# A hybrid decoder layer on one core: 1/rms in the projection's input, evictions on ScalarE, tail copies on GpSimd, log1p as a product of quadratics

## Chip, cores, metric

One Trainium2 chip, one core. The metric is the device time of one execution in microseconds; the time before is 2660.73 us, the median of three runs (2657.97 to 2662.61). The profile is of one execution. Engines: PE is TensorE (PEld its weight loads), DVE is VectorE, ACT is ScalarE, POOL is GpSimd, SP issues the DMAs.

## What is computed

One decoder layer over 16 meta tokens and 2048 real tokens of width 1024, in float32, batch 1:

```
h    = rmsnorm(x, norm1_g);  proj = h @ w_in            # one projection, 3608 columns
qkv  = silu(causal_conv(proj[q, k, v], conv_w))         # 4 taps, 1536 channels
gated delta rule, 4 heads of 128 (chunked)              # log decay: -exp(a_log) * softplus(...)
g    = log_sigmoid(glr @ gla_w2 + gla_b) / 16           # glr: 16 columns of proj; g: 256 channels
gated linear attention, 4 heads (chunked, cumsum of g)
x    = x + concat(rmsnorm(o) * silu(gate)) @ w_out
x    = x + square(relu(rmsnorm(x) @ w_up)) @ w_down     # 4096 wide
out  = rmsnorm(x, final_norm_g)
```

The log of a sigmoid is computed as min(x, 0) - log1p(e) with e = exp(-|x|), and log1p on [0, 1] as e times a polynomial of degree 9.

## The kernel before

Matmuls keep float32 accuracy by splitting each operand into a high and a low part: `mm3` (lines 117 to 119) issues three matmuls, high times high, high times low and low times high. `wchunk` (L95) loads 256 rows of weights, ScalarE casts the high part `whi` (L101), and VectorE, or GpSimd for two chunks of four in the projection, subtracts it for the low part `wlo` (L102). `split` (L107) does the same for activations (`hh` and `hl`, lines 112 and 113).

The program runs in this order: projection of token blocks 0 and 1 (`phase_a`, blocks of 512 tokens), the scans over pairs of chunks of 128 tokens woven with blocks 2 and 3, and then the output projection and the MLP (`phase_c`) of blocks 0, 1 and last 2 and 3 together. The blocks are numbered 0 to 3, as in the code. A scheduler sets each engine's order from the dependences, priorities and its own estimates of durations, so that work of the scans stands between the matmuls of the projection. Every engine works its own queue in order.

`phase_a` has eight groups per block (`group`, L232). A group takes four PSUM banks `pa`, four chunks of weights (kk) and 24 matmuls of each chunk (four banks, two rows of 128 weights, three parts): 96 matmuls. First one token group, then three convolution groups (`conv_group`, q, k and v channels on the partitions), one group for q and k of the gated linear attention, and three token groups. At a group's end each bank is evicted: token groups by ScalarE with 1/rms as a scale on the partition (`evac_tok`, L336), channel groups by VectorE with 1/rms along the free dimension, `rb` (`evac_c`, L409, tile `craw`; `evac_g`, L375, tile `gqk`). 1/rms comes from `stats` (L191), in the same block's first group, since the input itself is only multiplied by the gain (`normless`, L168). After a convolution group, for each bank, VectorE copies three columns in front of the new block from `tails` and three of its end into `tails` (lines 416 and 417), ScalarE does the first tap (L419, tile `cy`) and VectorE the other three (L421), then a silu.

The pool of banks has four buffers. The jobs of `decays` (L352) run in small parts between the groups and take a bank each: `pglr`, `pgc`, `pgr`, `pgla`. So at a group's end TensorE goes on only when banks have been evicted, and the buffers go round. `gla_decay` (L310) evaluates log1p (L157) by Horner's rule on VectorE: one product and nine steps of 512 columns.

The scan's inverse of 32 x 32 blocks is a chain of some 60 VectorE instructions per pair of chunks (`inv_t`, `inv_v`, lines 564 and 570), followed by two levels of small matmuls with copies between them (`wt`, lines 586 and 606).

## Time and profile before

| | |
|---|---|
| median of three runs | 2660.73 us |
| span of the profiled execution | 2658.3 us |
| TensorE busy | 2569.2 us (97%) |
| VectorE busy | 1625.0 us (61%) |
| ScalarE busy | 905.4 us (34%) |
| GpSimd busy | 475.8 us (18%) |
| mean granted TensorE clock | 0.986 |

The profiled execution's own time is its span and the little that lies around it; the page gives only the span, and the median of the runs stands 2.4 us above it. The share of busy time is an average over stages. Rows name a line of the kernel, the engine, the operation and the tiles (out<-in, buffer numbers left out). A wait names the instruction that ended last.

### The profile page before, as it was taken

How to read it: one execution, taken by the hardware profiler on the slowest of the kernel's cores; microseconds unless marked ns; L12 is line 12 of the kernel's file. 1: busy time of each engine (PE TensorE's matmuls, PEld its weight loads, DVE VectorE, ACT ScalarE, POOL GpSimd, SP SyncE). 2: the span in 40 equal slices, each digit the busy share in tenths (PEclk: the TensorE clock that was granted, in tenths of full speed). 3: DMA queues.
4: the chain of work that ended last, by engine and by line, in shares of the span. 5: the costliest groups of instructions: out<-in, count | busy, mean ns of one | idle time of the engine just before them, and what ended most of it. 6: DMA issues, size and time to landing. Idle time of an engine off the chain costs nothing.

```text
span 2658.3 us, 35430 instructions
## 1 busy us (share of the span) xinstructions
PE 2569.2 (97%) x13426; PEld 2127.1 (80%) x13426; DVE 1625.0 (61%) x3122; ACT 905.4 (34%) x1850; POOL 475.8 (18%) x385
## 2 busy tenths in 40 slices
PE   8999999999899999999998999999999999999998
PEld 6788688789678778888786888888888888888887
DVE  4777866985984875857679567555453343233335
ACT  4344345345334433334353243333321122112212
POOL 2123123223222321102044020101230000000003
PEclk9999999999999999999999999999999999999999
DMA  5264455355346323334363343253211111111111
GB/s 180 102 214 146 139 152 182 111 187 174 126 154 201 103 89 124 104 106 127 115 208 94 100 121 105 86 175 108 98 48 48 48 48 48 48 48 48 48 48 64
DMA packets 187122, 297.30 MB, mean 112 GB/s; under 512 B 33584, under 2 KB 116104, under 8 KB 186952
## 3 DMA queue, kind: packets, MB, share of 16 engines
q1 hardware_dynamic: 186952, 295.05, 35.5%
q8 instruction: 105, 1.72, 0.3%
q14 instruction: 65, 0.53, 0.1%
HBM read 244.62 MB, written 50.37 MB: 111 GB/s over the span
## 4 chain that ended last, share of the span: by engine, by line
PE 63%; DVE 9%; issue 2%; DMA 2%; POOL 1%; ACT 0%; SPq 0%; POOLq 0%; DVEq 0%; ACTq 0%
PE pc L119 18%; PE pc L118 18%; PE pc L117 18%; PE pa L117 2%; PE pa L118 2%; PE pa L119 2%; DVE wlo L102 1%; DVE inv_t L564 1%; DVE inv_v L570 1%; PE pks L650 1%; DVE l1p L163 0%; PE po L661 0%; PE pu L664 0%; PE po L660 0%; PE py L654 0%
## 5 line engine op out<-in xcount | busy, mean ns | idle before, releaser
L101 ACT CAST whi<-wraw 128x1024 fp32r<-128x1024 f32 (+1 forms) x344 | 346.9, 1009 | 1067.8 <-PE pc L118 813.0
L102 DVE TENSOR_TENSOR wlo<-wraw,whi 128x1024 fp32r<-128x1024 f32 (+1 forms) x280 | 344.8, 1232 | 576.3 <-ACT whi L101 575.2
L118 PE MATMUL pc<-avl,whi 128*128 128x512 f32 (+1 forms) x1056 | 413.1, 391 | 2.5 <-DVE avl L110 2.4
L117 PE MATMUL pc<-avh,whi 128*128 128x512 f32 (+1 forms) x1056 | 397.4, 392 | 12.2 <-DVE acc L974 12.0
L119 PE MATMUL pc<-avh,wlo 128*128 128x512 f32 (+1 forms) x1056 | 406.7, 389 | 0.0
L117 PE MATMUL pc<-h2h,whi 128*128 128x512 f32 x1024 | 402.0, 393 | 2.8 <-DVE acc L896 2.8
L118 PE MATMUL pc<-h2l,whi 128*128 128x512 f32 x1024 | 402.7, 393 | 0.0
L119 PE MATMUL pc<-h2h,wlo 128*128 128x512 f32 x1024 | 399.1, 396 | 1.1 <-DVE wlo L102 1.1
L117 PEld LDWEIGHTS pc<-avh,whi 128*128 128x128 f32 x1056 | 199.6, 189 | 57.3 <-issue 13.3
L118 PEld LDWEIGHTS pc<-avl,whi 128*128 128x128 f32 x1056 | 199.4, 189 | 47.1 <-DVE avl L110 4.8
L119 PEld LDWEIGHTS pc<-avh,wlo 128*128 128x128 f32 x1056 | 199.4, 189 | 42.8
L883 POOL TENSOR_TENSOR tot<-tot,sqk 128x512 f32<-128x512 f32 (+1 forms) x63 | 84.5, 1347 | 824.3 <-ACT sqk L882 822.5
L117 PEld LDWEIGHTS pc<-h2h,whi 128*128 128x128 f32 x1024 | 192.5, 188 | 46.1 <-DVE acc L896 4.1
L119 PEld LDWEIGHTS pc<-h2h,wlo 128*128 128x128 f32 x1024 | 192.3, 188 | 44.4 <-DVE wlo L102 1.9
L118 PEld LDWEIGHTS pc<-h2l,whi 128*128 128x128 f32 x1024 | 192.4, 188 | 42.6
L974 DVE TENSOR_TENSOR acc<-acc,pc 128x512 f32<-128x512 f32 x240 | 162.2, 685 | 104.3 <-PE pc L119 101.9
L102 POOL TENSOR_TENSOR wlo<-wraw,whi 128x780 fp32r<-128x780 f32 (+1 forms) x64 | 142.9, 2233 | 433.2 <-ACT whi L101 345.0
L117 PE MATMUL pa<-hh,whi 128*128 128x512 f32 x512 | 206.6, 405 | 4.2 <-ACT whi L101 2.3
L118 PE MATMUL pa<-hl,whi 128*128 128x512 f32 x512 | 202.7, 396 | 0.0
L119 PE MATMUL pa<-hh,wlo 128*128 128x512 f32 x512 | 188.8, 400 | 2.0 <-DVE wlo L102 1.2
L117 PE MATMUL pa<-whi,hh 128*128 128x390 f32 x512 | 167.8, 357 | 13.8 <-ACT hh L112 11.2
L118 PE MATMUL pa<-wlo,hh 128*128 128x390 f32 x512 | 180.4, 354 | 0.1
(274 smaller groups left out, 4079.7 us busy)
## 6 DMA issues: line engine op xcount, KB each, us to landing
wraw<-in_wup_dram SPq DMA_DIRECT2D x96, 512.0 KB, 3.6
wraw<-in_wdn_dram SPq DMA_DIRECT2D x96, 512.0 KB, 3.6
wraw<-in_wch_dram SPq DMA_DIRECT2D x64, 512.0 KB, 3.7
wraw<-in_wtk_dram SPq DMA_DIRECT2D x64, 390.0 KB, 3.9
qkv_d<-cy SPq DMA_DIRECT2D x48, 256.0 KB, 2.3
kqv<-qkv_d SPq DMA_DIRECT2D x16, 768.0 KB, 5.3
wraw<-in_wo_dram SPq DMA_DIRECT2D x24, 512.0 KB, 3.6
xk<-in_xT_dram SPq DMA_DIRECT2D x32, 256.0 KB, 4.2
```

What stands on the lines that cost most here:

```text
L101: A.copy(out=hi[:, :, 0:n], in_=raw[:, :, 0:n])
L102: eng.tensor_tensor(out=lo[:, :, 0:n], in0=raw[:, :, 0:n], in1=hi[:, :, 0:n].bitcast(F32), op=ALU.subtract)
L117: T.matmul(o, lhsT=ah, rhs=bh, start=first, stop=False)
L118: T.matmul(o, lhsT=ah, rhs=bl, start=False, stop=False)
L119: T.matmul(o, lhsT=al, rhs=bh, start=False, stop=last)
L564: V.tensor_tensor(out=t, in0=vv[:, 0:c, c : c + 1].broadcast_to([L, c, n]), in1=vv[:, c : c + 1, c + 1 : w].broadcast_to([L, c, n]), op=AL ...
L570: V.tensor_tensor(out=vv[:, 0:c, c + 1 : w], in0=vv[:, 0:c, c + 1 : w], in1=t, op=ALU.add)
L650: T.matmul(h4(pk)[:, h, :], lhsT=kg[:, h, :], rhs=S[:, h, :], start=True, stop=True)
L883: eng.tensor_tensor(out=tot, in0=tot, in1=sq, op=ALU.add)
L974: V.tensor_tensor(out=x, in0=x, in1=banks[j][i], op=ALU.add)
```

## The change

In blocks 1 to 3 the input is multiplied by gain and 1/rms on VectorE before it is split, so that evictions need no factor; ScalarE evicts channel banks there. The row sums of the next block are taken after the fourth group of the block before. GpSimd copies the convolution's tails, with two buffers of tails. log1p of the linear attention's gates becomes a product of one linear and four quadratic factors: ScalarE squares, VectorE multiplies. Block 0 keeps its evictions.

```diff
+_roots = np.roots(LOG1P[::-1])
+LR = float(_roots[np.abs(_roots.imag) < 1e-9].real[0])
+LA = [float(-z.real) for z in _roots if z.imag > 1e-9]
+LB = [float(z.imag**2) for z in _roots if z.imag > 1e-9]
+LC = LOG1P[-1]
...
+    lsc = [(-LC) ** 0.5, 1.0, 1.0, 1.0]
+    lbias = const("lbias", [128, 4])
+    for i in range(4):
+        G.memset(lbias[:, i : i + 1], lsc[i] * LA[i])
...
+    norms = {}
+    def stats(b):
+        rt = wk.tile([128, 4], F32, name="rt", tag="rt")
+        rb = wk.tile([128, 512], F32, name="rb", tag="rb")
...
+        A.copy(out=rb, in_=pb)
+        norms[b] = rt, rb
...
+        told, tnew = tails[b % 2], tails[(b + 1) % 2]
...
-        def normless(k):
+        def moving(k):
             if k not in hT:
                 xk = t512("xk")
                 nc.sync.dma_start(out=xk, in_=I["xT"][b, k])
                 hT[k] = act("h")
-                split(xk, *hT[k], g1[:, k : k + 1])
+                if meta:
+                    split(xk, *hT[k], g1[:, k : k + 1])
+                else:
+                    V.scalar_tensor_tensor(out=xk, in0=xk, scalar=g1[:, k : k + 1], in1=norms[b][1], op0=ALU.mult, op1=ALU.mult)
+                    split(xk, *hT[k])
             return hT[k]
...
-                x = t512("glx")
-                V.tensor_scalar(out=x[:, 0:n], in0=px[:, 0:n], scalar1=gb[:, j : j + 1], scalar2=None, op0=ALU.add)
-                e = t512("gle")
...
-                l = yield from log1p(e[:, 0:n], 128, [512] if n == 512 else [n], f"l1p_{n}")
-                V.scalar_tensor_tensor(out=x[:, 0:n], in0=x[:, 0:n], scalar=0.0, in1=l[:, 0:n], op0=ALU.min, op1=ALU.subtract)
-                V.tensor_tensor_scan(out=dst[j], data0=rmask[:, 0:n], data1=x[:, 0:n], initial=0.0, op0=ALU.mult, op1=ALU.add)
+                x = dst[j]
+                V.tensor_scalar(out=x, in0=px[:, 0:n], scalar1=gb[:, j : j + 1], scalar2=None, op0=ALU.add)
+                e, y = tl("gle"), tl("gly")
+                A.activation(out=e, in_=x, func=AF.Abs)
+                A.activation(out=e, in_=e, func=AF.Exp, scale=-1.0)
+                V.scalar_tensor_tensor(out=y, in0=e, scalar=-LR, in1=e, op0=ALU.add, op1=ALU.mult)
+                for i in range(4):
+                    yield False
+                    sq = tl("gls")
+                    A.activation(out=sq, in_=e, func=AF.Square, scale=lsc[i], bias=lbias[:, i : i + 1])
+                    V.scalar_tensor_tensor(out=y, in0=sq, scalar=lsc[i] ** 2 * LB[i], in1=y, op0=ALU.add, op1=ALU.mult)
+                V.scalar_tensor_tensor(out=y, in0=x, scalar=0.0, in1=y, op0=ALU.min, op1=ALU.add)
+                V.tensor_tensor_scan(out=x, data0=rmask[:, 0:n], data1=y, initial=0.0, op0=ALU.mult, op1=ALU.add)
...
         def evac_tok(t, pt):
             st = av("tok")
-            A.activation(out=st[:, 0:NTOK], in_=pt[:, 0:NTOK], func=AF.Copy, scale=rt[:, t : t + 1])
+            if meta:
+                A.activation(out=st[:, 0:NTOK], in_=pt[:, 0:NTOK], func=AF.Copy, scale=norms[0][0][:, t : t + 1])
+            else:
+                A.copy(out=st[:, 0:NTOK], in_=pt[:, 0:NTOK])
...
         def evac_g(j, pt):
...
+                A.activation(out=st[:, 0:TB], in_=pt, func=AF.Copy, scale=scale)
...
             def evac_c(j, pt):
                 raw = av("craw")
-                V.tensor_tensor(out=raw[:, 3 : TB + 3], in0=pt, in1=rb, op=ALU.mult)
+                if meta:
+                    V.tensor_tensor(out=raw[:, 3 : TB + 3], in0=pt, in1=norms[0][1], op=ALU.mult)
+                else:
+                    A.copy(out=raw[:, 3 : TB + 3], in_=pt)
...
-                V.tensor_copy(out=raw[:, 0:3], in_=tails[:, m, :])
-                V.tensor_copy(out=tails[:, m, :], in_=raw[:, TB : TB + 3])
+                G.tensor_copy(out=raw[:, 0:3], in_=told[:, m, :])
+                if b + 1 < NB:
+                    G.tensor_copy(out=tnew[:, m, :], in_=raw[:, TB : TB + 3])
...
         group(I["wch"][3], 512, True, evac_g, done_g, 512 if meta else 0, meta_g)
+        if b + 1 < NB:
+            stats(b + 1)
...
-                m = tail.tile([128, 512], F32, name="mixk", tag="mixk", bufs=4) if tail else t512("mixk")
+                m = tail.tile([128, 512], F32, name="mixk", tag="mixk", bufs=3) if tail else t512("mixk")
```

The scheduler orders the whole program anew. Three places show what moved.

VectorE, end of the second convolution group of block 2, before (`pa` are the group's banks, `cy` the taps of the group before, `inv` the inverse of the chunk pair):

```order
L102 TENSOR_TENSOR wlo_5290<-wraw_5287,whi_5289 128x1024
L564 TENSOR_TENSOR inv_t_4196<-inv_v_4195 32x220
L426 SCALAR_TENSOR_TENSOR cy_5079<-cth_5084,cy_5079 128x512
L411 TENSOR_TENSOR craw_5219<-pa_5088,rb_4667 128x512
L416 COPY craw_5221<-tails_137 128x3
L570 TENSOR_TENSOR inv_v_4195<-inv_v_4195,inv_t_4196 32x11x20
L411 TENSOR_TENSOR craw_5221<-pa_5089,rb_4667 128x512
L416 COPY craw_5223<-tails_137 128x3
L417 COPY tails_137<-craw_5219 128x3
L411 TENSOR_TENSOR craw_5223<-pa_5090,rb_4667 128x512
```

The same group's end in the change, on ScalarE:

```order
L112 CAST whi_5221<-wraw_5219 128x1024
L467 ACTIVATE cth_5118<-cy_5113 128x512
L112 CAST whi_5322<-wraw_5320 128x1024
L452 COPY craw_5253<-pa_5122 128x512
L452 COPY craw_5255<-pa_5123 128x512
L452 COPY craw_5257<-pa_5124 128x512
L112 CAST whi_5355<-wraw_5353 128x1024
L452 COPY craw_5259<-pa_5125 128x512
L351 ACTIVATE gle_5267<-bb_4921 128x512
```

The evictions of this group went from VectorE's queue, between taps and inverse, to ScalarE's, three of them ahead of the cast of the next group's second chunk (`whi_5355`).

GpSimd in the change, between the weights of this group and those of the next (`wlo_5356` is the low part of that second chunk; before, the rows `wlo` of the two groups followed each other there):

```order
L113 TENSOR_TENSOR wlo_5191<-wraw_5188,whi_5190 128x1024
L457 COPY craw_5255<-tails0_142 128x3
L459 COPY tails1_143<-craw_5253 128x3
L457 COPY craw_5257<-tails0_142 128x3
L459 COPY tails1_143<-craw_5255 128x3
L457 COPY craw_5259<-tails0_142 128x3
L459 COPY tails1_143<-craw_5257 128x3
L457 COPY craw_5454<-tails0_142 128x3
L113 TENSOR_TENSOR wlo_5356<-wraw_5353,whi_5355 128x1024
```

Seven tail copies came in between two weight subtractions.

VectorE at the start of block 2 in the change (`xk` is the input, `rb` 1/rms, `Sg`, `gqg` and `f_u` belong to the scan; before, the two `hl` followed on their casts without a product ahead):

```order
L211 SCALAR_TENSOR_TENSOR xk_4735<-xk_4735,g1_135,rb_2846 128x512
L211 SCALAR_TENSOR_TENSOR xk_4745<-xk_4745,g1_135,rb_2846 128x512
L827 SCALAR_TENSOR_TENSOR Sg_124<-Sg_124,gall_3949,pgu_3987 64x128 x4
L783 TENSOR_SCALAR gqg_4346<-gqg_4346,eb_4341 128x64 x2
L93 TENSOR_SCALAR f_u_4002<-ms_3997 128x4
L211 SCALAR_TENSOR_TENSOR xk_4779<-xk_4779,g1_135,rb_2846 128x512
L121 TENSOR_TENSOR hl_4738<-xk_4735,hh_4737 128x512
L121 TENSOR_TENSOR hl_4748<-xk_4745,hh_4747 128x512
```

Each `xk` is now multiplied first, then cast by ScalarE, then subtracted.

## Rows read from the trace of the kernel before

**Rows 1.** The page's busy table: busy us, share of the span, instructions.
```profile
PE 2569.2 (97%) x13426; PEld 2127.1 (80%) x13426; DVE 1625.0 (61%) x3122; ACT 905.4 (34%) x1850; POOL 475.8 (18%) x385
```
**Rows 2.** Busy time of each engine by stretch: the four blocks of the projection, and the time from the output projection on. Columns: stretch in us, its length, busy us of each engine with its instructions, mean granted TensorE clock, DMA share, GB/s.
```profile
0.00:240.00 240.00, 223.53 (x1236) 187.71 (x1237) 161.76 (x379) 104.03 (x212) 61.85 (x52) 0.97 0.52 166
240.00:430.00 190.00, 176.76 (x969) 148.56 (x969) 143.95 (x289) 73.01 (x140) 51.85 (x38) 0.96 0.48 149
430.00:640.00 210.00, 200.55 (x1195) 174.83 (x1195) 170.09 (x363) 95.00 (x233) 64.80 (x47) 0.98 0.51 158
640.00:850.00 210.00, 194.30 (x1079) 164.71 (x1079) 159.10 (x321) 81.22 (x165) 50.22 (x35) 0.97 0.48 150
850.00:2600.00 1750.00, 1727.90 (x8644) 1409.38 (x8644) 962.60 (x1715) 538.63 (x1074) 226.23 (x193) 1.00 0.30 92
```
**Rows 3.** What TensorE waited for, 0 to 850 us: us in total, times, longest.
```profile
PE pa L117 <- ACT hh L112: 11.2, 6, 6.2
PE pr L614 <- DVE wt L606: 5.7, 2, 3.0
PE pgc L301 <- DVE craw L411: 5.4, 3, 2.5
PE pgla L322 <- DVE craw L411: 4.3, 2, 2.2
...
PE pa L117 <- DVE tails L417: 1.9, 4, 0.7
```
**Rows 4.** VectorE in order of time at the end of the second convolution group of block 2: start us, us, instruction, and the idle time before it if there was any.
```profile
506.54 1.21 DVE L102 TENSOR_TENSOR wlo<-wraw,whi 128x1024 fp32r<-128x1024 f32 x1
...
508.57 0.67 DVE L411 TENSOR_TENSOR craw<-pa,rb 128x512 f32<-128x512 f32 x1
509.17 1.70 DVE L416 COPY craw<-tails 128x3 f32<-128x3 f32 x1
...
511.09 0.67 DVE L411 TENSOR_TENSOR craw<-pa,rb 128x512 f32<-128x512 f32 x1
```
**Rows 5.** TensorE at the same place, the same columns.
```profile
506.14 0.39 PE L118 MATMUL pa<-hl,whi 128*128 128x512 f32 x1
506.37 0.39 PE L119 MATMUL pa<-hh,wlo 128*128 128x512 f32 x1
509.30 0.40 PE L301 MATMUL pgc<-g,tri 128*128 128x16 f32 x2 [2.54 <-DVE craw L411]
511.81 2.07 PE L322 MATMUL pgla<-glrT,w 16*128 16x512 f32 x2 [2.12 <-DVE craw L411]
513.81 0.80 PE L117 MATMUL pa<-hh,whi 128*128 128x512 f32 x1
```
**Rows 6.** ScalarE at the same place, the same columns.
```profile
506.87 1.03 ACT L101 CAST whi<-wraw 128x1024 fp32r<-128x1024 f32 x1
514.73 0.63 ACT L326 ACTIVATE gle<-glx 128x512 f32<-128x512 f32 x1 [6.83 <-DVE glx L324]
```
**Rows 7.** GpSimd at the same place.
```profile
507.98 2.87 POOL L102 TENSOR_TENSOR wlo<-wraw,whi 128x1024 fp32r<-128x1024 f32 x1 [11.57 <-ACT whi L101]
```
**Rows 8.** Busy time by stretch, columns as in rows 2: six stretches around evictions of channel groups, and the two of 358 and 784 us around the last levels of the inverse.
```profile
262.00:270.00 8.00, 6.36 (x35) 4.68 (x34) 7.81 (x23) 3.91 (x6) 1.97 (x2) 1.00 0.44 150
286.00:306.00 20.00, 15.02 (x75) 9.96 (x75) 17.01 (x32) 6.14 (x10) 2.72 (x3) 0.74 0.37 119
...
505.00:517.00 12.00, 7.34 (x20) 4.50 (x19) 11.90 (x31) 3.44 (x5) 2.87 (x1) 0.72 0.47 153
560.00:573.00 13.00, 11.24 (x93) 8.53 (x91) 12.53 (x17) 5.42 (x10) 4.40 (x3) 1.00 0.61 201
690.00:699.00 9.00, 6.58 (x36) 4.85 (x35) 8.60 (x22) 3.81 (x6) 2.84 (x2) 1.00 0.47 152
718.00:729.00 11.00, 7.72 (x37) 4.80 (x36) 9.58 (x21) 4.07 (x7) 2.55 (x2) 0.69 0.50 154
...
358.00:372.00 14.00, 10.52 (x66) 9.55 (x64) 11.60 (x18) 3.40 (x6) 1.85 (x1) 0.76 0.46 135
784.00:799.00 15.00, 11.28 (x63) 10.29 (x62) 12.25 (x19) 2.06 (x4) 1.98 (x1) 0.77 0.39 115
```
**Rows 9.** Groups of VectorE's instructions by line and shape, 0 to 850 us: out<-in, sizes, count | busy us, mean ns of one | idle before.
```profile
L163 DVE SCALAR_TENSOR_TENSOR l1p<-l1p,gle 128x512 f32<-128x512 f32 x72 | 60.0, 833 | 1.6
...
L411 DVE TENSOR_TENSOR craw<-pa,rb 128x512 f32<-128x512 f32 x48 | 32.5, 678 | 1.4 <-PE pa L119 1.3
...
L113 DVE SCALAR_TENSOR_TENSOR hl<-xk,g,hh 128x512 fp32r<-128x512 f32 x32 | 26.1, 837 | 9.0 <-ACT hh L112 8.8
...
L417 DVE COPY tails<-craw 128x3 f32<-128x3 f32 x48 | 16.3, 351 | 0.0
L416 DVE COPY craw<-tails 128x3 f32<-128x3 f32 x48 | 12.4, 266 | 0.0
```
**Rows 10.** The same of ScalarE: the first tap with its scale on the partition, and an eviction of a full bank by a plain copy in the scans.
```profile
L419 ACT ACTIVATE cy<-craw,convw 128x512 f32<-128x512 f32 x48 | 34.1, 711 | 9.1 <-DVE craw L411 7.5 <-DVE glx L329 1.4
...
L814 ACT COPY mixt<-pmix 128x512 f32<-128x512 f32 x9 | 5.2, 581 | 2.8 <-PE pmix L812 2.8
```
**Rows 11.** The same of GpSimd: a product of two tensors in 128 columns, and a small memset.
```profile
L734 POOL TENSOR_TENSOR gqg<-gl,eb 128x128 f32<-128x128 f32 x14 | 9.0, 661 | 9.4 <-PE pog L770 9.4
...
L93 POOL MEMSET mhalf<- 128x16 f32 x1 | 0.1, 111 | 0.0
```

More of the change, by code (lines that the diff above doesn't have):

```diff
@@ L38 @@
 ]
+_roots = np.roots(LOG1P[::-1])
[3 more added lines that the diff above has]
+LC = LOG1P[-1]
+assert len(LA) == 4 and LC < 0
 @with_exitstack
@@ L150, in hybrid_kernel @@
     gv_m = bp.tile([NMETA, 512], F32, name="gv_m")
+    norms = {}
+    def stats(b):
+        rt = wk.tile([128, 4], F32, name="rt", tag="rt")
+        rb = wk.tile([128, 512], F32, name="rb", tag="rb")
+        ss = wk.tile([128, 4], F32, name="ss", tag="ss")
+        for t in range(4):
+            xt = k4("xt")
+            r0 = b * TB + t * 128
+            nc.sync.dma_start(out=xt, in_=I["x"][r0 : r0 + 128, :])
+            A.activation(out=xt, in_=xt, func=AF.Square, accum_out=ss[:, t : t + 1])
+        rsqrt(wk, "n1", ss, 128, 4, 1.0 / D, EPS, rt)
+        pb = mm("rstd_bc")
+        for t in range(4):
+            dg = wk.tile([128, 128], F32, name="dg", tag="dg")
+            G.tensor_scalar(out=dg, in0=ident, scalar1=rt[:, t : t + 1], scalar2=None, op0=ALU.mult)
+            T.matmul(pb[:, t * 128 : (t + 1) * 128], lhsT=ones, rhs=dg, start=True, stop=True)
+        A.copy(out=rb, in_=pb)
+        norms[b] = rt, rb
     def phase_a(b, kc, late=None):
@@ new lines, in first_stats @@
+        def first_stats():
+            late(0)
+            stats(0)
+            xm = k4("xm")
+            G.memset(xm, 0.0)
+            for q in range(4):
+                nc.sync.dma_start(out=xm[32 * q : 32 * q + NMETA, :], in_=I["meta"])
+            ssm = wk.tile([128, 1], F32, name="ssm", tag="ssm", bufs=1)
+            A.activation(out=xm, in_=xm, func=AF.Square, accum_out=ssm)
+            rm = rsqrt(wk, "n1m", ssm, 128, 1, 1.0 / D, EPS)
+            for half in range(2):
+                c0 = 64 * half
+                V.tensor_tensor(
+                    out=eq[:, half, :], in0=ident[:, c0 : c0 + NMETA], in1=ident[:, c0 + 32 : c0 + 32 + NMETA], op=ALU.add
+                )
+            V.tensor_scalar(out=eq, in0=eq, scalar1=rm, scalar2=None, op0=ALU.mult)
@@ L376, in evac_g @@
             st = av("gqk")
-            V.scalar_tensor_tensor(out=st[:, 0:TB], in0=pt, scalar=0.125 if j < 2 else 1.0, in1=rb, op0=ALU.mult, op1=ALU.mult)
+            scale = 0.125 if j < 2 else 1.0
+            if meta:
+                V.scalar_tensor_tensor(out=st[:, 0:TB], in0=pt, scalar=scale, in1=norms[0][1], op0=ALU.mult, op1=ALU.mult)
+            else:
+                A.activation(out=st[:, 0:TB], in_=pt, func=AF.Copy, scale=scale)
             return st
@@ L390, in meta_c @@
                 )
-                V.tensor_copy(out=tails[:, 4 * i : 4 * i + 4, :], in_=raw_m[:, 4 * i : 4 * i + 4, NMETA:])
+                V.tensor_copy(out=told[:, 4 * i : 4 * i + 4, :], in_=raw_m[:, 4 * i : 4 * i + 4, NMETA:])
                 y = wk.tile([128, 4, NMETA], F32, name="ym", tag="ym")
@@ L1022, in hybrid_kernel @@
     convw = small("convw", [128, 12, 4])
-    tails = small("tails", [128, 12, 3])
+    tails = [small(f"tails{i}", [128, 12, 3]) for i in range(2)]
     rmask = small("rmask", [128, 512])
```

48 lines of the change are left out of this document (9 added, 39 removed).

## The prediction

> **What bounds the kernel now.** [...] Second, the stretches [rows 2]: from 850 us on TensorE is busy for 1727.9 of 1750 us at a mean granted clock of 1.00, so the later stages give nothing. The four blocks of the projection with the scans woven in, 0 to 850 us, leave 16.5, 13.2, 9.5 and 15.7 us idle at clocks of 0.96 to 0.98, while VectorE is busy for 76 to 81% of blocks 1 to 3. So what is saved in these blocks goes straight into the end, since all that follows is TensorE's own work. Third, who TensorE waited for there [rows 3]: VectorE's evictions `craw`, its tail copies and its `wt` copies lead, with the split inputs `hh`.
>
> Fourth, one such place in order of time: the end of the second convolution group of block 2. The last matmul of the group starts at 506.37 us; the next matmul needs a bank that VectorE evicts, and starts at 509.30, the one after it at 511.81, each behind a `craw` [rows 5]. VectorE was working off a queue: a weight subtraction, then the first eviction only at 508.57, then a copy of three columns that took 1.70 us, and the second eviction at 511.09 [rows 4]. That copy lay beside GpSimd's 2.87 us subtraction [rows 7] and ended with it. ScalarE meanwhile did nothing for 6.83 us [rows 6]. After the two waits the clock stood at the lower level for a part of the stretch: 0.72 in the mean of 505 to 517 us [rows 8].
>
> **What these places cost.** Six stretches around evictions, 262:270, 286:306, 505:517, 560:573, 690:699 and 718:729, leave 1.64 + 4.98 + 4.66 + 1.76 + 2.42 + 3.28 = 18.7 us idle; their clocks of 0.74, 0.72 and 0.69 lose 0.26 x 20 + 0.28 x 12 + 0.31 x 11 = 12.0 us more [rows 8]. Together 31 us, of which I take 30, since idle time at the low clock is counted twice. Two more stretches, 358:372 and 784:799, are waits for `wt`, the last levels of the triangular inverse: 3.5 + 3.7 idle and 3.4 + 3.4 of clock, 14 us [rows 8].
>
> **The change, part by part.**
> *Evictions.* In blocks 1 to 3, 12 `craw` and 4 `gqk` of a block leave VectorE: 16 x 0.678 = 10.8 us a block [rows 9]. ScalarE gets them at the price of its own 512-column eviction of another bank, 0.581 us [rows 10], 9.3 us a block. In the new order ScalarE's three first evictions stand right behind two weight casts and a tanh, with nothing of VectorE's ahead. TensorE ends bank 0 twelve matmuls, 12 x 0.23 = 2.8 us [rows 5], before the group's end, so 0.58 us on a free ScalarE is hidden: cost 0. If the cover is gone, because ScalarE is in a 1.03 us cast [rows 6] and another eviction, it is up to 2 us at each of 9 group ends: bounds 0 to 18, I take 3, nearest to the idle ScalarE of [rows 6]. [...]
> *1/rms into the input.* In exchange, blocks 1 to 3 get 8 products of the input with gain and 1/rms on VectorE, at the price of `hl`, 0.837 us [rows 9], 6.7 us a block; the split behind them stays two instructions of unchanged length. It lies beside TensorE's last group, but at a block's start TensorE already waits for `hh`, 11.2 us in all [rows 3], and the product now stands in that chain: 3 x 0.84 = 2.5 us; bounds 0 and all eight in line, 20 us. The DMAs of `xk` keep their places in SP's queue to within a few rows. The row sums of the next block move a block ahead, so their 4 DMAs and squares compete with the fourth group's casts instead of the first group's: 0.
> *Conv tails.* 24 copies a block leave VectorE: 12 x (0.351 + 0.266) = 7.4 us [rows 9]. GpSimd gets them between 0.11 us (a small memset) and 0.66 us (128 columns of two inputs) [rows 11]; three columns are nearest to the memset, I take 0.25 us. In the new order seven of them stand in front of GpSimd's weight subtraction of the next group: 1.8 us. That subtraction can start 1.03 us after the group's end and takes 2.87 [rows 6, 7]; TensorE reaches the chunk after 24 matmuls, 5.5 us, so 1.6 us of slack are just used up: I take 2 us in all. At 0.66 us a copy it would be late by 3 us at 9 places, 27 us: bounds 0 to 27.
> *log1p.* Each of 8 blocks of gates loses five VectorE instructions net (13 become 8): 2 x 5 x 0.833 = 8.3 us a block [rows 9]. ScalarE gets 8 squares a block with a bias on the partition, at 0.711 us as `cy` with its scale [rows 10], 5.7 us, beside idle time.
> So VectorE loses 10.8 + 7.4 + 8.3 - 6.7 = 19.8 us in blocks 1 to 3 and 15.7 us in block 0, 75 us of the 635 it works up to 850 us [rows 2]. A lag of VectorE of some 5 us at a group's end (506.4 to 511.8 [rows 4, 5]) should go by this.
> *`wt`.* The chain of the inverse stays on VectorE, and fewer log1p steps of 0.833 us [rows 9] stand between its copies, but other work of VectorE moves up and the order puts the levels elsewhere: bounds 0 and 14, I take half, 7 us.
>
> **Sum**: 30 + 7 - 3 - 2.5 - 2 = 29.5 us less. The profiled execution spans 2658.3 us; 2.4 us lie around it to the median of 2660.7, which I take to stay. So 2658.3 - 29.5 + 2.4 = **2631 us**.
>
> **Rivals.**
> *A. The waits move to ScalarE (chance 0.22).* ScalarE's queue is in order: its evictions now wait for TensorE, and the next chunk's cast stands behind three of them, the row sums' squares behind that. For it: 3 x 0.58 before a cast at each of 9 ends is 16 us. Against it: in block 2 ScalarE is busy for 95 of 210 us [rows 2] and would go to 110. Half to all of the first price and no gain at `wt` leaves 0 to 18 us: about 2652 us, reaching to no change.
> *B. GpSimd and VectorE lock each other out (chance 0.10), slower.* The row of 1.70 us for three columns, ended by GpSimd's subtraction, shows the lock in one direction [rows 4, 7]. The other way, every tail copy on GpSimd would wait for a VectorE instruction of up to 0.84 us; seven in front of the subtraction make 5.9 us, the low part comes at 1.03 + 5.9 + 2.87 = 9.8 instead of 5.5 us, 4.3 us late, and with 1.7 us for the clock behind each wait (half of the 3.4 us a stretch loses at most) 9 x 6.0 = 54 us come on top of the 37 won: 2678 us. It decides from some 0.6 us a copy on: then 9 x (7 x 0.57 + 1.03 + 2.87 - 5.5 + 1.7) = 37 us. [...]
> *C. More goes than the six places (chance 0.13).* With 75 us less on VectorE both `wt` places and small waits in block 0 go as well: 45 to 55 us, 2610 us. Against it: new orders bring new waits.
> *D. The edit misses the cause (within A).* The next group's third and fourth banks are those that `pgc` and `pgla` held, and VectorE still empties these. If its lag comes from its other work (a weight's low part stands ahead in [rows 4]), half of the 30 us stays: 2646 us.
>
> **How the numbers follow.** Forecast (15 to 44 us less) 0.52, A 0.22, B 0.10, C 0.13, and 0.03 for a later stage that the new order lengthens. 0.2%, 5.3 us, is about what a measurement of this kernel can tell from no change. Faster by more: forecast and C, and about two thirds of A, 0.79; within: 0.08, the rest of A; slower: B and the last, 0.13. The range takes in C's end and A up to no change: 2606 to 2660 us; it leaves out B and a few in 100 below.
>
> **What would show it.** In the profile after, right: no wait of TensorE for `craw` on VectorE in blocks 1 to 3, `craw` on ScalarE at about 0.58 us, block 2's clock near 1.00 between 480 and 530 us, tail copies under 0.4 us, the output projection's first matmul some 30 us earlier. Wrong: waits of TensorE for `whi` or for GpSimd's `wlo` of over 1 us at group ends (A, B), or the same 3 us waits for `wt`. The forecast is wrong if the sum of idle time up to the output projection stays above 45 us.

## The result, and the profile after

The change is slower: 2670.77 us median of four runs (2668.53 to 2672.92) against 2661.67 us of the kernel before (2657.97 to 2664.95) on the same chip; ratio 1.0041, 95% interval [1.0028, 1.0054]. The forecast was 2631 us (2606 to 2660).

The busy table of the change, as [rows 1]: VectorE was relieved of 50 us, and ScalarE and GpSimd took on 45 and 39 us, yet TensorE is busy longer, with the same 13,426 instructions.

```profile
PE 2581.5 (97%) x13426; PEld 2123.8 (80%) x13426; DVE 1574.9 (59%) x2952; ACT 950.6 (36%) x1938; POOL 515.1 (19%) x473
```

The stretches of the change, as [rows 2] and, the last two, as [rows 8] and around it:

```profile
0.00:240.00 240.00, 208.00 (x1134) 169.20 (x1135) 139.06 (x306) 103.37 (x216) 65.43 (x80) 0.96 0.50 155
240.00:430.00 190.00, 185.18 (x1044) 156.79 (x1043) 134.45 (x257) 90.49 (x165) 60.33 (x60) 1.00 0.49 148
430.00:640.00 210.00, 199.79 (x1188) 173.37 (x1185) 167.28 (x343) 106.28 (x259) 80.05 (x76) 0.98 0.52 163
640.00:850.00 210.00, 202.27 (x1119) 172.64 (x1118) 146.27 (x270) 99.37 (x191) 52.12 (x42) 0.99 0.53 161
850.00:2600.00 1750.00, 1731.72 (x8613) 1402.87 (x8612) 953.00 (x1710) 531.90 (x1071) 236.22 (x195) 1.00 0.29 91
480.00:530.00 50.00, 46.71 (x206) 36.24 (x205) 47.23 (x100) 24.92 (x48) 19.39 (x25) 0.97 0.47 161
505.00:517.00 12.00, 11.72 (x49) 8.63 (x48) 11.79 (x22) 6.75 (x10) 4.47 (x9) 1.00 0.41 140
```

TensorE's idle time in the first four stretches is now 32.0, 4.8, 10.2 and 7.7 us: blocks 1 to 3 won 15.6 us, and 505:517 us went from 4.66 us idle at a clock of 0.72 to 0.28 us at 1.00. But block 0 lost 15.5 us, so the sum stands at 54.8 us as before (54.9), above the 45 us that the prediction named as the sign of a wrong forecast. From 850 us on TensorE is busier than before and does fewer instructions in the same time.

What TensorE waited for, 0 to 850 us, as [rows 3] (us in total, times, longest):

```profile
PE pmeta L272 <- DMA wraw<-in_wtk_dram: 9.0, 2, 8.2
PE pq L532 <- DVE at L581: 7.0, 1, 7.0
PE pa L128 <- ACT whi L112: 6.5, 6, 2.4
PE pa L128 <- ACT hh L123: 6.5, 1, 6.5
PE pa L128 <- ACT hh L120: 3.5, 2, 1.7
...
PE pa L128 <- ACT rb L182: 2.3, 1, 2.3
```

The waits for VectorE's `craw` and `tails` have left the list, and those for `wt` fell from 7.8 to 0.2 us. New at its head are a wait for a weight load and one for `at`, a tile of the scans that VectorE makes; the longest of both (8.2 and 7.0 us) fall before 240 us. The first is in block 0, whose sixth group (the second token group) goes like this on TensorE (start us, us, instruction, idle before):

```profile
145.68 0.39 PE L130 MATMUL pa<-hh,wlo 128*128 128x512 f32 x1
145.91 0.96 PE L288 MATMUL pmeta<-eq,msb 128*128 128x16 f32 x8
146.80 0.59 PE L272 MATMUL pmeta<-wraw,hm 128*32 128x73 f32 x24
155.61 0.47 PE L272 MATMUL pmeta<-wraw,hm 128*32 128x73 f32 x8 [8.22 <-DMA wraw<-in_wtk_dram]
...
159.61 0.64 PE L181 MATMUL rstd_bc<-dg,ones 128*128 128x128 f32 x2
159.90 0.67 PE L128 MATMUL pa<-whi,hh 128*128 128x390 f32 x1
...
171.72 0.44 PE L128 MATMUL pa<-whi,hh 128*128 128x390 f32 x1 [2.27 <-ACT rb L182]
```

The fifth group ends at 145.9 us. Then come the meta tokens' products of the whole sixth group, which need all four of its weight chunks, then a product of the row sums (`rstd_bc`), and only at 159.90 the group's first own matmul. Its fourth bank starts at 171.72, when ScalarE has copied the row sums' bank (`rb`). In SP's queue the four loads of the row sums (`xt`) stand among the weights; the last weight load shown is the one that the 8.22 us wait ends with:

```profile
137.74 0.55 SPq L108 DMA_DIRECT2D wraw<-in_wtk_dram  x1
138.34 1.08 SPq L174 DMA_DIRECT2D xt<-in_x_dram  x2
141.09 0.55 SPq L108 DMA_DIRECT2D wraw<-in_wtk_dram  x1
...
144.68 2.73 SPq L174 DMA_DIRECT2D xt<-in_x_dram  x2
...
151.18 0.57 SPq L108 DMA_DIRECT2D wraw<-in_wtk_dram  x1
```

These loads hardly delay the weights. The same weight load in the kernel before, and in the run with log1p and tail copies below (third line: that chunk's meta products on TensorE):

```profile
149.06 1.23 SPq L97 DMA_DIRECT2D wraw<-in_wtk_dram  x2
```
```profile
152.16 0.55 SPq L110 DMA_DIRECT2D wraw<-in_wtk_dram  x1
166.39 0.34 PE L265 MATMUL pmeta<-wraw,hm 128*32 128x73 f32 x8
```

There the load is 2 us earlier and 1 us later than in the change. With log1p and tail copies TensorE takes the fourth chunk's meta products between the group's own matmuls, at 166.39 us, and does not wait for it. So the 8.2 us come from TensorE's order in the change.

In the kernel before, the sixth group's first eviction on ScalarE started at 168.57 us, here at 180.95.

The second new wait is at the start of block 1, still before 240 us: VectorE's new product of the input waits for its load, and `at`, which TensorE needs, stands behind it in VectorE's queue (two lines of VectorE, one of TensorE):

```profile
232.90 0.75 DVE L211 SCALAR_TENSOR_TENSOR xk<-xk,g,rb 128x512 f32<-128x512 f32 x1 [5.25 <-DMA xk<-in_xT_dram]
233.56 0.69 DVE L581 TENSOR_TENSOR at<-pqk,gm 128x512 f32<-128x512 f32 x1
234.31 1.11 PE L532 MATMUL pq<-ident,kqv 128*128 128x128 f32 x4 [6.96 <-DVE at L581]
```

The edited instructions, 0 to 850 us, as [rows 9 to 11]: ScalarE's eviction, VectorE's product of the input, GpSimd's tail copies (busy us, mean ns of one):

```profile
L452 ACT COPY craw<-pa 128x512 f32<-128x512 f32 x36 | 20.6, 584 | 8.5 <-PE pa L130 8.3
L211 DVE SCALAR_TENSOR_TENSOR xk<-xk,g,rb 128x512 f32<-128x512 f32 x24 | 20.1, 842 | 10.1 <-DMA xk<-in_xT_dram 9.6 <-DVE xk L211 0.4
L457 POOL COPY craw<-tails 128x3 f32<-128x3 f32 x48 | 15.5, 344 | 1.3 <-DVE tails L429 1.2
L459 POOL COPY tails<-craw 128x3 f32<-128x3 f32 x36 | 14.7, 408 | 64.3 <-DVE craw L450 32.3 <-ACT craw L452 30.8 <-PE pmeta L272 1.2
```

The output projection's first matmul, in the kernel before and in the change:

```profile
848.89 1.19 PE L117 MATMUL pc<-mxh,whi 128*128 128x512 f32 x4 [1.02 <-ACT mxh L112]
```
```profile
843.07 0.79 PE L128 MATMUL pc<-mxh,whi 128*128 128x512 f32 x1 [2.26 <-ACT mxh L123]
```

So 5.8 us are won up to there, and 14 are lost behind it, since the span is 8.4 us longer. A part of both is work that only moved: TensorE does 4,445 instructions up to there instead of 4,475, and 34 more in the stage behind. It waits no longer there than before, but its matmuls are slower: the same group, 970 to 1340 us, in the kernel before and in the change (busy us, mean ns):

```profile
L117 PE MATMUL pc<-h2h,whi 128*128 128x512 f32 x218 | 85.3, 391 | 0.0
```
```profile
L128 PE MATMUL pc<-h2h,whi 128*128 128x512 f32 x214 | 85.0, 397 | 0.0
```

### The profile page after: what moved, and what is told of

It reads as the page before. It is cut to its first block, busy times and chain, and to the rows that moved or that the text cites. A ratio compares the mean times of both kernels' runs of the same rounds, so it can differ in the third digit from the quotient of the medians.

```text
span 2666.7 us, 35433 instructions
## 1 busy us (share of the span) xinstructions
PE 2581.5 (97%) x13426; PEld 2123.8 (80%) x13426; DVE 1574.9 (59%) x2952; ACT 950.6 (36%) x1938; POOL 515.1 (19%) x473
## 4 chain that ended last, share of the span: by engine, by line
PE 72%; DVE 9%; DMA 2%; issue 1%; ACT 1%; POOL 0%; SPq 0%; POOLq 0%; DVEq 0%; ACTq 0%
PE pc L128 19%; PE pc L129 19%; PE pc L130 19%; PE pa L130 3%; PE pa L129 3%; PE pa L128 3%; DVE inv_v L614 2%; DVE inv_t L608 1%; DVE wlo L113 1%; DVE cy L463 1%; DVE acc L994 1%; DMA gl<-gla_d 1%; DMA qkv_d<-cy 1%; DMA gate_d<-gth 0%; PE pu L708 0%
```

## The experiments

Each ratio is against runs of the kernel before on the same chip; a difference in us goes by the medians.

**One part at a time.** Three explanations of the loss are tested first: Q, the row sums' loads in SP's queue; S, ScalarE's queue; M, something in the later stages.

Row sums after the sixth group:

```diff
-        if b + 1 < NB:
-            stats(b + 1)
         group(I["wtk"][1], ...)
+        if b + 1 < NB:
+            stats(b + 1)
```


> The change, with one edit: the row sums of the next block are issued after the sixth group (second token group) instead of after the fourth (before it). Theory Q (queue): in the change the four 512 KB loads of the row sums stand in SP's in-order queue between the weights of the sixth group of block 0 and wait there for a buffer; TensorE waits 8.2 us for a weight load and the clock falls, and block 0 ends 12 us late, the start of block 1 19 us late. By Q the weights come first again, the 8 us wait goes, the stretch 0 to 240 us loses at most 20 us idle instead of 32, the output projection starts 10 to 15 us earlier than in the change (near 830 us), and the time is 2655 to 2660 us, 0.998 to 1.0 of before. Rival S (ScalarE): the loss comes from evictions and squares in ScalarE's queue ahead of the weight casts; the number of squares is unchanged, so the time stays at 2666 to 2672 us, 1.002 to 1.004. Rival M (a later stage): of the 8 us lost in the end, 14 arise behind the output projection's start and stay whatever block 0 does, so that from its first matmul to the end it is again 1823 us and not 1809.

Measured: 2666.44 us, 1.003 [1.002, 1.0041]. Q failed as put: the weight wait went, and another came, as TensorE's order of time shows:

```profile
183.51 0.80 PE L181 MATMUL rstd_bc<-dg,ones 128*128 128x128 f32 x2 [12.93 <-POOL dg L180]
```

The row sums' products stand in TensorE's in-order queue, and their loads come late there too. The time lies in the range of S, so this run does not rule S out. M held: 1826 us from the output projection's first matmul to the end of the span, after 1823 in the change and 1809 before.

Log1p alone: the new `gla_decay` in the kernel before.

> The kernel before with only the new log1p (13 VectorE instructions a block of gates become 8, ScalarE squares). The prediction: VectorE gives up 8.3 us a block, about 33 us up to 850 us; of the 30 us at evictions this is 33 of 75 us of relief, so if relief of VectorE is what counts, 5 to 13 us less: ratio 0.995 to 0.998. Theory Q: nothing lost here, since SP's queue keeps its order; 0.995 to 1.000. Rival S: eight squares a block at 0.71 us in ScalarE's queue delay weight casts: 1.000 to 1.003, with waits of TensorE for whi of over 4 us in all.

Measured: 2639.81 us, 0.9925 [0.9913, 0.9937], 19 us faster, more than the 5 to 13 expected; S, which needed 1.000 or more, is out for this part. TensorE's idle time up to the output projection fell from 54.9 to 43.9 us, but its waits for `craw` and `tails` on VectorE are nearly as long as before, 12.9 us in all after 14.8; the longest of them here:

```profile
PE pa L130 <- DVE tails L440: 5.5, 4, 2.7
PE pgc L314 <- DVE craw L434: 2.8, 3, 1.4
PE pglr L333 <- DVE craw L434: 2.7, 2, 2.5
```

Tail copies alone:

```diff
-                V.tensor_copy(out=raw[:, 0:3], in_=tails[:, m, :])
-                V.tensor_copy(out=tails[:, m, :], in_=raw[:, TB : TB + 3])
+                G.tensor_copy(out=raw[:, 0:3], in_=told[:, m, :])
+                if b + 1 < NB:
+                    G.tensor_copy(out=tnew[:, m, :], in_=raw[:, TB : TB + 3])
```


> The kernel before with only the tail copies on GpSimd and two buffers of tails (and the two small cuts of buffers in the last stage that make room for it: av of the last pool 4 columns shorter, three mixk buffers instead of four). VectorE gives up 7.4 us a block; by relief alone 2 to 7 us less: ratio 0.997 to 0.999. Rival B of the prediction (GpSimd waits for VectorE, each copy 0.6 us or more, seven ahead of a weight subtraction): 1.005 to 1.015 with waits for wlo of 10 us or more. Rival M: if the last stage of the change is slow because of these cuts of buffers, the time from the first matmul of the output projection to the end is 10 to 14 us longer than the 1809 us of before here too.

Measured: 2663.31 us, 1.0013 [1.0, 1.0026]. B is out. From the output projection's first matmul on it loses 9 us, with order and waits nearly as before.

The 1/rms part alone: the change with log1p and tail copies as before.

> The kernel before with only the 1/rms part: row sums a block ahead (after the fourth group, as in the change), 1/rms multiplied into the input of blocks 1 to 3, channel banks evicted by ScalarE; log1p and the tail copies stay on VectorE as before. Theory Q: the loads of the row sums stand in SP's queue among the weights of the sixth group, so this part carries the loss of block 0: 0:240 loses 10 us or more over before, while the waits for craw in blocks 1 to 3 go; the time is 2660 to 2672 us, 1.000 to 1.004. Rival: the part wins what the prediction said (evictions away) and the loss comes from log1p or GpSimd: 0.990 to 0.996.

Measured: 2675.61 us, 1.0064 [1.005, 1.0077]. This part has the largest loss, at an address that costs time too, as shown below; the sixth group of block 0 ends at 191.7 us (before 169.0).

**The same instructions at other addresses.** In the middle stage of the slow ones the matmuls that read `h2` (the MLP's first product) start every 232 to 234 ns, in the kernel before and with log1p alone every 227 (medians, from the starts in the timeline). What differs is where the buffers lie. Addresses here and below are bytes in a partition, as the built program places its buffers.

```diff
-    tails = small("tails", [128, 12, 3])
+    tails = small("tails", [128, 14, 3])
```


> The kernel before, with the tails tile 24 bytes longer per partition (rounded to 32): every engine's instructions and their order stay as they are, only the buffers behind it, the split activations among them, lie 32 bytes further on. Theory L (layout): where the weights (stationary) and the activations (moving) lie at the same address modulo 64, a 512-column matmul starts every 227 to 230 ns in the median (before, and log1p alone); where they differ by 32, every 232 to 235 (the change, tails alone, fold alone). By L this kernel gets 3 to 5 ns more for some 3400 matmuls of the middle stage and 1500 to 3000 of the projection: 12 to 20 us, time 2671 to 2679 us, ratio 1.004 to 1.008, the median interval 232 ns or more. Rival C (cuts of buffers): the later stages of the change lose time by the shorter av and the third mixk buffer, which this kernel does not have: no change, 0.999 to 1.001, and 227 to 229 ns.

Measured: 2671.88 us, 1.0049 [1.0037, 1.0062]: 13 us for 32 bytes, with every engine's order unchanged. The row shown above of before and change, here:

```profile
L117 PE MATMUL pc<-h2h,whi 128*128 128x512 f32 x224 | 88.7, 396 | 0.0
```

The change with 32 bytes more:

```diff
-    tails = [small(f"tails{i}", [128, 12, 3]) for i in range(2)]
+    tails = [small(f"tails{i}", [128, 12 + 2 * i, 3]) for i in range(2)]
```


> The change, with one of the tails tiles 24 bytes longer: order and instructions unchanged, weights and activations at the same address modulo 64 again. Theory L: 3 to 5 ns less for each 512-column matmul, 12 to 20 us less than the change: 2650 to 2658 us, ratio to before 0.996 to 1.000, and the stretch from the output projection's first matmul to the second one's some 986 us instead of 997. Rival C: as the change, 2666 to 2672 us, 1.003 to 1.005.

Measured: 2666.74 us, 1.0034 [1.0022, 1.0047]. The rule modulo 64 failed: the difference of the addresses went from 96 to 128, and the medians stayed at 232 ns. Log1p and tails together, with the same two extra columns (a difference of 192), failed for the same reason:

> The kernel before with log1p and the tail copies of the change, no 1/rms in the input (row sums and evictions as before), laid out so that weights and activations are at the same address modulo 64. If theory L and the runs of the parts add: log1p alone was 18.6 us faster, tails alone 4.9 slower with the other address and so 7 to 12 faster without it: 2627 to 2636 us, ratio 0.988 to 0.992. If the tail copies on GpSimd win nothing by themselves: as log1p alone, 2637 to 2643 us, 0.992 to 0.994.

Measured: 2655.98 us, 0.9991 [0.9982, 1.0]. And the row sums in two parts:

```diff
         rsqrt(wk, "n1", ss, 128, 4, 1.0 / D, EPS, rt)
+        norms[b] = rt, rb
+    def spread(b):
+        rt, rb = norms[b]
         pb = mm("rstd_bc")
...
         group(I["wtk"][1], ...)
+        if b + 1 < NB:
+            stats(b + 1)
         group(I["wtk"][2], ...)
+        if b + 1 < NB:
+            spread(b + 1)
```


> The change with the 32 bytes as above, and the row sums in two parts: loads, squares and the power after the sixth group, the four products that spread 1/rms over the partitions after the seventh. Theory Q2 (TensorE's own queue): the products of the row sums stand in TensorE's in-order queue and, with their loads late, hold it for 6.8 to 12.9 us in block 0 (fold alone, sums later); taken apart, that wait goes: 0:240 loses at most 20 us idle instead of 32, and the time is 10 to 17 us under the change with the 32 bytes: 2635 to 2645 us, 0.990 to 0.995. Rival H: block 0's loss comes back at the start of block 1, where the input waits for 1/rms (waits for hh or rb of 6 us or more): 2648 to 2658 us, 0.996 to 1.000.

Measured: 2665.61 us, 1.0034 [1.0019, 1.0049]. The sixth group is quick; the seventh then waits 7.0 us for a weight's cast, behind the squares in ScalarE's queue. At both later places an in-order queue waits for the row sums' loads, TensorE's above and ScalarE's here.

Sorted by the difference of the addresses of weights and activations, the 512-column matmuls of all runs that read `h2`, 945 to 1330 us, gave medians of 227 ns where it is 0 modulo 512 and of 230 to 234 elsewhere. The next four test that.

```diff
-        t = wk.tile(shape, F32, name=name, bufs=1)
+        t = (bp if name in ("ealog", "dtb", "gb") else wk).tile(shape, F32, name=name, bufs=1)
```


> The change with three small constants (96 bytes per partition in all) moved from the work pool to the scan pool: same instructions in the same order, the activations lie 96 bytes lower, so that the addresses of stationary and moving operand agree modulo 512 and not only modulo 64. In the runs so far the 512-column matmuls of the middle stage start every 227 ns in the median where the difference of the addresses is 0 modulo 512 (before, log1p alone) and every 230 to 234 for every other difference (before with 32 bytes: 13 us slower). Theory L512: 227 ns here too, the time from the output projection's first matmul to the second one's is 984 to 988 us instead of 997, and the whole is 2650 to 2658 us, 0.996 to 1.000 of before. Rival P: it is the absolute place of the buffers or something else that happened to go with it: as the change, 2666 to 2672 us, 1.003 to 1.005.

Measured: 2656.38 us, 0.9989 [0.998, 0.9997]: 14 us less than the change, same order of instructions. In the profiled executions 5.5 of 12.6 us lie ahead of the output projection's first matmul (837.6 us) and 7.1 behind it. The same line on the split row sums:

> The change with the row sums in two parts (loads, squares, power after the sixth group; the products that spread 1/rms after the seventh) and with the 96 bytes moved. Sums split with the other address was 2665.6 us. By L512: 12 to 16 us less, 2648 to 2655 us, 0.995 to 0.999. If, with the address out of the way, block 0's loss is the rest of it, this is also 3 to 8 us under the change with the 96 bytes. Rival P: 2663 to 2669 us.

Measured: 2652.76 us, 0.9973 [0.9962, 0.9984]. Log1p and tails, with `tails1` moved in this way:

> The kernel before with log1p and tail copies of the change, one tails tile moved to the scan pool so that the difference of the addresses is 0 modulo 512. With another difference it was 2656.0 us. By L512 16 to 20 us less: 2636 to 2642 us, 0.991 to 0.994, about the same as log1p alone (0.9925), so that the tail copies on GpSimd would be worth nothing by themselves. If the tail copies do win 7 to 12 us: 2626 to 2634 us, 0.988 to 0.991. Rival P: 2653 to 2660 us.

Measured: 2641.9 us, 0.9929 [0.9917, 0.9942]: no more than log1p alone. The kernel before with `convw`, `ealog` and `dtb` moved:

> The kernel before with three small constants (256 bytes) moved from the work pool to the scan pool: same instructions in the same order, the difference of the addresses is 256 modulo 512, still 0 modulo 64, 128 and 256. If only 512 counts: as with 32 bytes, 8 to 13 us slower, 1.003 to 1.005, median interval 230 to 234 ns. If the modulus is 256 or less: no change, 0.999 to 1.001, 227 to 229 ns.

Measured: 2658.72 us, 0.9993 [0.9981, 1.0004]; the row reads 391 ns as before. So 256 is as good as 0; 128 was not. Rival P is out as well: activations at 224 modulo 512 were slow with weights at 192 (32 bytes more) and quick with weights at 224 (log1p alone, and the change with the 96 bytes moved).

**The rest of the loss, with the address out of the way.**

```diff
-        pb = mm("rstd_bc")
+        pb = ps("rstd_bc") if b == 1 else mm("rstd_bc")
```


> The change with the 96 bytes moved, and in block 0 the products that spread 1/rms of block 1 take a bank of the scan's pool instead of one of the four banks of the projection's groups. Theory B (bank): in the change TensorE's order at the end of block 0's fifth group is: all meta products of the sixth group, which need all its four chunks of weights, then the row sums' products, then three of the group's banks, and the fourth bank only behind the copy of the row sums' bank. With the other bank the sixth group's first matmuls stand right behind the fifth group. By B the sixth group ends near 168 us instead of 182.8, and the time is 10 to 16 us under the 2656.4 of the change with the 96 bytes: 2640 to 2646 us, 0.993 to 0.995. Rival Q3 (loads late whatever the bank): the row sums' loads come late behind buffers, TensorE or ScalarE waits for them in its queue as in the runs with later or split sums; the sixth or seventh group loses 10 us or more again: 2652 to 2658 us, 0.997 to 1.000.

Measured: 2651.84 us, 0.9972 [0.9963, 0.9981]: 4.5 us of the expected 10 to 16. The sixth group's matmuls now follow the fifth at once, but TensorE still waits for its last weights, and its first eviction starts at 177.73 us (TensorE's wait, and the one in SP's queue, 160 to 163.5 us, that their load stands behind):

```profile
172.05 0.34 PE L272 MATMUL pmeta<-wraw,hm 128*32 128x73 f32 x8 [4.07 <-DMA wraw<-in_wtk_dram]
```
```profile
SPq L469 <- DVE cy L468: 7.4, 1, 7.4
```

The bank is a smaller part; Q3 lies on the way of the larger, by a detour. The row sums' loads themselves have left SP's queue by 148.4 us. But the last weights are loaded only at 164.30, behind a store that waits for the convolution's `cy`, and the first tap of that `cy` (at 154.82; at 148.41 with log1p and tail copies) stands in ScalarE's queue behind the squares, for whose loads ScalarE waited 2.0 and 1.3 us.

1/rms into the input only from block 2 on:

```diff
-                if meta:
+                if b < 2:
                     split(xk, *hT[k], g1[:, k : k + 1])
...
-        if b + 1 < NB:
+        if 0 < b < NB - 1:
             stats(b + 1)
```


> The change with the 96 bytes moved, but 1/rms goes into the input only in blocks 2 and 3 (counted from 0); block 1 keeps its row sums in its own first group and its factors in the evictions. Theory B: block 0's 16.7 us go, and block 1, which won nothing measurable over log1p with tails (both took 199 to 200 us), loses nothing: 2640 to 2646 us, 0.993 to 0.995. Rival: the loss is one of row sums ahead wherever they stand; then it moves to block 1 and block 2 as well, and the time is 2650 to 2657 us, 0.997 to 0.999.

Measured: 2644.02 us, 0.994 [0.9926, 0.9955]. Block 0's loss is gone (first eviction of the sixth group at 166.38 us); what is left is log1p's gain and no more. TensorE's idle time up to the output projection is 43.8 us here, 45.2 with log1p and tail copies and 43.9 with log1p alone, in the one execution profiled of each, though the waits for VectorE's `craw` fell from 11.1 us (log1p and tail copies) to 4.4: other waits took their place.

> The kernel before with the tail copies on GpSimd, one tails tile in the scan pool so that the operands' addresses differ by 0 modulo 256 as in the kernel before. With another difference it was 1.0013. By the address alone (1.0049 for 32 bytes in the kernel before) 0.996 to 0.997, 2648 to 2652 us: then the copies themselves are worth 8 to 11 us. If they are worth nothing, as log1p with and without them says (0.9929 and 0.9925): 0.999 to 1.001.

Measured: 2655.25 us, 0.9981 [0.997, 0.9992], between the two: some 5 us by themselves, 2 to 8 by the interval.

> The kernel before with the 1/rms part alone (row sums a block ahead, product into the input, ScalarE evictions), operands' addresses differing by 0 modulo 256. With another difference it was 1.0064. By the address alone 1.001 to 1.002, 2661 to 2665 us. Its own loss at the sixth group of block 0 (22 us there with the other address) stays, so it is not faster than before; were it 0.995 or less, that loss would hang on the address too.

Measured: 2666.44 us, 1.0028 [1.0017, 1.0039], as the address would have it, or a little more.

Only the row sums a block ahead (the run before without the product and with the evictions of the kernel before):

> The kernel before with only the row sums taken a block ahead (after the fourth group, as in the change); input, evictions, log1p and tail copies as before, operands' addresses differing by 0 modulo 256. Theory Q3 (the row sums' place): the sixth group of block 0 ends near 183 to 191 us instead of 169, as in all kernels with the sums there; nothing is won elsewhere: 2668 to 2680 us, 1.004 to 1.008. Rival: the loss needs the input's product or ScalarE's evictions beside it: 2656 to 2662 us, 0.999 to 1.001. The prediction's step said 0.

Measured: 2666.46 us, 1.003 [1.0018, 1.0041]; 8 us, under the 10 expected. Its waits, 140 to 260 us:

```profile
PE pmeta L272 <- DMA wraw<-in_wtk_dram: 10.3, 1, 10.3
PE rstd_bc L181 <- POOL dg L180: 6.8, 1, 6.8
PE pa L128 <- ACT hh L123: 5.3, 1, 5.3
```

The sixth group ends at 193.1 us, 24 us late, and most of that comes back in the later blocks: block 0's last projection matmul starts 26 us later than before, block 3's 4 us. So the move alone costs all that the 1/rms part costs (1.0028).

Log1p alone with all matmul operands of the later stages at one address modulo 256:

```diff
-        return q.tile([128, TB + 4], dt, name=name, tag="av", bufs=8)
+        return q.tile([128, TB + 64 if q is wk else TB], dt, name=name, tag="av", bufs=8)
...
-                ssm = wk.tile([128, 1], F32, name="ssm", tag="ssm", bufs=1)
+                ssm = wk.tile([128, 57], F32, name="ssm", tag="ssm", bufs=1)[:, 0:1]
...
-            row = wk.tile([16, 128], F32, name="gcrow", tag="gcrow", bufs=1)
+            row = wk.tile([16, 144], F32, name="gcrow", tag="gcrow", bufs=1)
...
-                m = tail.tile([128, 512], F32, name="mixk", tag="mixk", bufs=4) if tail else t512("mixk")
+                m = tail.tile([128, 512], F32, name="mixk", tag="mixk", bufs=3) if tail else t512("mixk")
```


> Log1p alone, with all buffers that the output projection and the MLP read as matmul operands (mx, av, h2 in both pools, weights in both pools) at the same address modulo 256: av tiles 60 columns longer, two small tiles longer, three mixk buffers. Log1p alone was 2639.8 us (0.9925). If the address rule holds for av too: its 512-column matmuls in the middle stage go from 235 to 239 ns in the mean to 228 to 231, some 1700 of them, 8 to 12 us, and 2 to 3 ns for some 2500 in the last stage, 5 to 8 us: 2620 to 2628 us, 0.985 to 0.988, the fastest version. If the rule is peculiar to h2: no change, 2637 to 2643 us, 0.992 to 0.994.

Measured: 2618.99 us, 0.9851 [0.9835, 0.9866]: 39 us faster than before and 52 than the change, the fastest version, and 21 us under log1p alone where 12 to 20 were expected. The stretch 2000 to 2500 us, in which TensorE is busy throughout, in the kernel before, in the change and here (columns as in [rows 2]):

```profile
2000.00:2500.00 500.00, 500.00 (x2156) 404.98 (x2155) 167.55 (x216) 93.43 (x129) 0.00 (x0) 1.00 0.16 47
```
```profile
2000.00:2500.00 500.00, 500.00 (x2151) 403.94 (x2150) 167.18 (x214) 91.55 (x125) 2.13 (x2) 1.00 0.15 48
```
```profile
2000.00:2500.00 500.00, 500.00 (x2208) 414.15 (x2207) 177.15 (x230) 101.11 (x142) 0.00 (x0) 1.00 0.15 49
```

A matmul takes 500 / 2156 = 231.9, 232.4 and 226.4 ns, at a granted clock of 1.00 in all three: in the first two, TensorE was busy 100% of the time and not at its peak.

## Why the prediction was wrong

It failed at two places that decide the sign, a step that was costed at nothing and a premise; and a rule of the sum, that a wait taken away is time won, failed beside them. Without row sums ahead in block 0 and with the address as before, the change takes 2644 us (0.994): the two places are 12 and 14 us.

*"The row sums of the next block move a block ahead ...: 0."* This step failed. By themselves the row sums, a block ahead, cost 8 us (1.003). In the change, with the address out of the way, the sixth group of block 0 takes 39.8 us from the fifth group's last matmul to its own, against 20.6 us for log1p and tails without it: 19 us, of which the blocks behind return some. The prediction named ScalarE's casts as what the loads and squares compete with. It did not follow the rest of the step: a bank out of four, and products in TensorE's own queue. In the new order the sixth group's meta products, with their need of all four chunks, stand ahead of its first matmul, and TensorE waits 8.2 us for the last chunk, though that chunk is loaded no later than with log1p and tail copies (151.18 and 152.16 us), where there is no such wait. That order could be read before the run; the places read were ends of convolution groups. What made the scheduler choose it was tested only for the bank, which returned 4.5 us.

*"So the later stages give nothing", "all that follows is TensorE's own work".* The premise was that the time from 850 us on is fixed. New small tiles moved the buffers behind them, and the matmuls that read `h2` there took 232 ns instead of 227 up to 1840 us; in the projection, too, the 512-column matmuls did: 1.0041 against 0.9989, 14 us. No rival had it; the 0.03 for a later stage "that the new order lengthens" had the place, but not the cause.

The terms of the sum, one by one:

- Evictions, 30 us: the `craw` waits are gone, ScalarE's eviction takes 0.584 us (0.581 forecast), the clock in 505:517 us is 1.00 (before, 0.72 in the mean, with 0.50 from 510 to 516 us). But the time did not follow. Log1p alone, which leaves the evictions and most of their waits where they were, wins 19 us, and with the tail copies and moved evictions on top nothing more is won: 0.9929, and 0.994 from block 2 on, with the idle time unchanged. The step "what is saved in these blocks goes straight into the end" took each wait as won with its cause; the "new orders bring new waits" of rival C held for the forecast too. Log1p had no term of its own in the sum; which waits its 19 us come from was not taken apart.
- `wt`, 7 us: of 7.8 us of these waits 0.2 are left, but `at`, another tile of the scans, went from 1.3 to 7.0 us.
- ScalarE's waits, 3 us (0 to 18): `whi` 6.5 us in six waits after 3.3 in three, about what was taken. Rival A did not decide.
- Product in the block-start chain, 2.5 us (0 to 20): the 11.2 us for `hh` [rows 3] hold 6.2 us of the kernel's very first load, so the block starts had 5.0 us, and 3.5 in the change. The price came elsewhere: the 7.0 us for `at` at the start of block 1, behind the product that waits for its load. With the row sums ahead alone, TensorE waits there 5.3 us for `hh` without any product, which speaks for the late load as the larger part.
- Tail copies, 2 us: 0.34 and 0.41 us a copy instead of 0.25, and the waits for GpSimd's `wlo` sum to 2.9 us in the change. Rival B, which needed 0.6 us a copy, did not come. Alone they win 5 us, on top of log1p none that can be told. What rival B reads as a lock from one copy is seen in both directions up to 850 us: in the kernel before, eight of VectorE's 96 tail copies took 1.22 to 2.38 us (median 0.15), each ending 0.02 to 0.03 us after a `wlo` on GpSimd; in the change, 32 of GpSimd's 84 took 0.35 to 1.55 us (median 0.19), each ending about 0.05 us after an instruction of VectorE. Why they end together is not shown.

A smaller slip, which decides nothing: "the 3.4 us a stretch loses at most" is 5.2 us in 286:306 by the prediction's own sum.

Without the two failed places the forecast would have been right in sign and too large by half, and that by luck: the terms of the sum are not what was won, log1p's 19 us are.

What stays open: why a difference of 0 modulo 256 makes matmuls quick (only that it does was shown), which step of the row sums makes the order that loses block 0's time, which waits log1p removes, and why the tail copies' 5 us vanish beside it.

## What to carry to other kernels

When a step is moved, list its instructions on each queue with what stands behind them at the new place, banks included: a load that is early in the program can be late in every queue (here, with the row sums after the sixth group, TensorE waited 12.93 us at their products). When a change adds or resizes a tile, compare the addresses of the matmul operands before and after, and give a version with unchanged order at another address before crediting a time to the edit; 13 us here came from 32 bytes. A stage at 100% busy and a granted clock of 1.00 can still be won from, as the 2208 instructions in 500 us after 2156 show: count its instructions per microsecond.

## What the runs showed of the hardware

Where weights and activations of the float32r matmuls lay at the same address modulo 256 (differences 0 and 256), 512-column matmuls followed each other every 227 ns; at differences of 32, 96, 128, 160 and 192 every 232 to 234 (matmuls that read `h2`, 945 to 1835 us, medians of each run). In the last stage, where some operands were in step and others, as half of the `h2` and most `av` tiles of all kernels but the last, were not, those in step took 230 to 231 ns too; with all in step, 227. The address of one operand against the other makes 2 to 3% of a 512-column matmul's time (227 against 232 to 234 ns), and 1.0049 of the whole in the kernel before with 32 bytes more, in the same order of instructions. Why it does is not shown.

In both traces, of the kernel before and of the change, every engine worked its queue in the program's order: TensorE's 13,426 instructions in each, VectorE's 3,122 and 2,952, and the 909 loads and stores in SP's queue, among others. TensorE's clock was granted at 1.00 or at 0.50 in them; 0.50 stood, for example, from 150 to 163 us in the change, from within the 8.22 us wait of the sixth group on.
